# A hybrid attention and state-space layer: where the bias table is built, and which token group writes the split weights back to memory

## The chip, the cores and the metric

The kernel runs on one core of a Trainium2 chip. The core has a matrix engine (PE, with its weight loads listed as PEld), a vector engine (DVE), an activation engine (ACT), a general engine (POOL), a queue engine (SP) that issues nearly all transfers here, and 16 DMA engines that carry them out. The metric is the device time of one execution in microseconds (us), lower is better.

## The reference, cut to what matters

One decoder layer runs over a prompt of 2048 tokens and 8 sample tokens that share the weights. All matrices are float32.

```python
h = rms_norm(x, norm1_w)
proj = h @ w_in                              # 1024 -> 2312 columns: q, k, v, z, x/B/C, dt
a = swa_prompt(q, k, v, attn_sinks, rel_bias)   # window 128, adds rel_pos_bias to the scores
s_out = ssm_mixer(z, xbc, dt_raw, ...)          # conv, chunked scan, gate, grouped norm
x = x + concatenate([a, s_out]) @ w_out
h2 = rms_norm(x, norm2_w)
x = x + (silu(h2 @ w_gate) * (h2 @ w_up)) @ w_down   # hidden width 2816
y = rms_norm(x, final_norm_w)
```

`rel_pos_bias` looks up, for each head, one number per distance between query and key (0 to 127). All blocks of the prompt use the same 128 x 256 bias per head.

## The kernel before, in words

**Groups.** The tokens go through the layer in six groups, one after another: 256 tokens, four times 384, and 256 + 8. A token group is held with the features on the partitions, and every projection is a chain of matmuls with 128 x 128 pieces of weight as the stationary operand and 256 or 384 tokens as the moving one.

**Split weights.** Each product is made of three matmuls (`mm3`): a weight is split into a high part in a rounded format and the low rest, and so are the activations; high x high, high x low and low x high are added. `weight` (L189) hands out one unit of weight, 128 x 512 values (some units of `wd` are 128 x 384), as a tile `w2` of 128 x 1024 that holds both parts. There are 196 units: 36 of `wi`, 16 of `wo`, 44 each of `wg` and `wu`, 56 of `wd`. A unit's 4 pieces take 12 matmuls (9 for 384 columns). At the first use, in the first group, the raw unit (256 KB) is loaded into `wraw` (4 buffers), ACT copies it to the high part (L197), DVE or POOL in turn subtracts (L200), and two steps later the split tile (512 KB) is written to a buffer in memory (L202). The other five groups load the 512 KB (L193) and split nothing. `w2` has 5 buffers, so a unit's tile is free again when its matmuls are done and, in the first group, when its write has landed too.

**Bias table.** `setup_bias` (L140) multiplies a one-hot matrix with the table `rel_bias` and gets `tabl`, 8 heads (on 8 partitions) x 384 values. It writes each head's row 128 times to a buffer `bscr` in memory (L152), 1.5 MB in all, from those 8 partitions, and then loads each head's 128 x 256 bias with a row step of 383 (L157), by which each row is shifted by one. It is called after the stage K of the first group.

**Stages and order.** Each group goes through stages: X (norm; I for the first group), A (x/B/C and dt columns, conv), K (k and v columns), B (q and z columns), P and Q (attention and scan, "mixers", one block of 128 tokens after the other), S (mixer output split), O (output projection), H (norm), F (feed-forward), Z (final norm). The `run` calls at the end write the stages in an interleaved order: A(0), K(0), B(0) and the mixers of group 0, A(1), B(1), O(0), K(1), then F(0) with the mixers of group 1 beside it, K(2), A(2), O(1), B(2), F(1), and so on; groups are numbered from 0. `later` puts a piece of work some steps behind. The tile framework then places the instructions: it sorts each engine's instructions by a priority and a timing model of its own, hands out the buffers, and sets all waits. So a small edit moves rows on every engine. Each engine takes its own rows in order.

**Where the stages lie in the profiled execution** (from the weight loads that SP issues): the units of A(0), K(0), B(0) are loaded raw from 3.7 to 134.3 us, O(0) from 141.7 to 244.5, F(0) from 245.7 to 588.8; the next stages' loads are K(2), A(2), O(1), B(2) from 594.2 to 705.8, F(1) from 707.9 to 1012.9, F(2) from 1128.0 on.

Of the kernel before, what the change touches and what calls it, by code (L numbers as in the profile page):

```python
# [10 lines left out]
F32 = mybir.dt.float32  # L11
# [6 lines left out]
P = 128  # L18
# [13 lines left out]
NH = 8  # L32
EPS = 1e-6
NEG = -1e30
TW = 384
# [37 lines left out]
def hymba(ctx: ExitStack, tc: tile.TileContext, I: dict, O: dict, groups):  # L73
# [14 lines left out]
    def T(shape, dtype=F32, tag=None, bufs=1):  # L88
        cnt[0] += 1
        nm = f"{tag}_{cnt[0]}"  # L90
        return sb.tile(shape, dtype, tag=tag, name=nm, bufs=bufs)

    def PS(tag):
        cnt[0] += 1
        return pp.tile([P, 512], F32, tag=tag, name=f"ps{tag}_{cnt[0]}", bufs=4)

    def DR(shape, tag, bufs=1):
        cnt[0] += 1
        return dr.tile(shape, F32, tag=tag, name=f"{tag}_{cnt[0]}", bufs=bufs)

    V, S, G, PE, SP = nc.vector, nc.scalar, nc.gpsimd, nc.tensor, nc.sync

    def mm(o, l, r, start=True, stop=True):
        PE.matmul(o, l, r, start=start, stop=stop)  # L104
# [29 lines left out]
    def setup_consts():  # L134
        for c, w, e in ((S_CB, 40, AF.Copy), (S_A, NH, AF.Exp), (S_AR, 4, AF.Exp)):
            S.activation(cols[:, c:c + w], cols[:, c:c + w], e, scale=0.5 if e == AF.Copy else 1.0)
        V.tensor_scalar(Ab, Ab, -1.0, None, ALU.mult)
        V.tensor_scalar(Ar, Ar, -1.0, None, ALU.mult)

    def setup_bias():  # L140

        rb = T([33, NH], tag="rb")
        V.memset(rb, NEG)
        SP.dma_start(rb[0:32, :], I["rel"])
        ps = PS("m")
        oh = T([33, TW], tag="m2", bufs=M2)
        SP.dma_start(oh, I["consts"][0:33, C_OH:C_OH + TW])
        mm(ps[0:NH, 0:TW], rb, oh)
        tabl = T([NH, TW], tag="m2", bufs=M2)
        V.tensor_copy(tabl, ps[0:NH, 0:TW])  # L150
        bscr = DR([NH, P * TW], "bscr")
        SP.dma_start(bscr.rearrange("h (q w) -> h q w", w=TW),  # L152
                     tabl.unsqueeze(1).broadcast_to([NH, P, TW]))
        V.tensor_copy(sbias[:, 1:P], tabl[:, 128:255])
        V.tensor_copy(sbias[:, 0:1], tabl[:, 255:256])
        for h in range(NH):
            SP.dma_start(bias[:, h, :],  # L157
                         bscr[h, 0:P * (TW - 1)].rearrange("(q w) -> q w", w=TW - 1)[:, P - 1:P - 1 + 2 * P])
# [16 lines left out]
    def later(n, fn):  # L175
        due.append((clock[0] + n, len(due) + cnt[0] * 1e-6, fn))

    def tick():
        clock[0] += 1
        now = sorted((d for d in due if d[0] <= clock[0]), key=lambda d: d[:2])  # L180
        due[:] = [d for d in due if d[0] > clock[0]]
        for d in now:
            d[2]()

    wn, kept = [0], {}

    def weight(name, at, w=512):  # L189
        t = T([P, 1024], F32R, tag="w2", bufs=5)[:, :2 * w]  # L190
        hi, lo = t[:, :w], t[:, w:]
        if (name, at) in kept:
            SP.dma_start(t.bitcast(F32), kept[name, at])  # L193
            return hi, lo
        raw = T([P, 512], tag="wraw", bufs=4)[:, :w]
        SP.dma_start(raw, I[name][at] if name != "wd" else I[name][:, at:at + w])
        S.activation(hi, raw, AF.Copy)  # L197
        e = G if wn[0] % 2 else V
        wn[0] += 1
        e.tensor_tensor(lo, raw, hi.bitcast(F32), ALU.subtract)  # L200
        d = kept[name, at] = DR([P, 2 * w], f"{name}{len(kept)}")
        later(2, lambda: SP.dma_start(d, t.bitcast(F32)))  # L202
        return hi, lo

    def std(name, u):

        r = []
        for h in range(2):
            hi, lo = weight(name, (u, h))
            r += [(hi[:, k * P:(k + 1) * P], lo[:, k * P:(k + 1) * P]) for k in range(4)]  # L210
        return r
# [752 lines left out]
    def stage_f(g):  # L964
# [5 lines left out]
        def down(c, end=False):  # L970
            fs, n = chunks[c], len(chunks[c]) * P

            for ms in ([[0, 1, 2], [3], [4], [5], [6], [7]] if end else [[m] for m in range(KT)]):
                w = [weight("wd", c_off[c] + m * n, n) for m in ms]
                ps = [PS("d") for m in ms]
                jobs = [(i, m) for i in range(len(fs)) for m in range(len(ms))]
                for i, m in sorted(jobs, key=lambda e: (e[0] == len(fs) - 1, e[1], e[0])):
                    wi = tuple(t[:, i * P:(i + 1) * P] for t in w[m])
                    s = fs[i] % (FC + 1)
                    mm3(ps[m][:, :N], wi, (hid3[:, s], hid3[:, FC + 1 + s]), 0, N, i == 0, i == len(fs) - 1)  # L980
                for m, p in zip(ms, ps):
                    V.tensor_tensor(x1[:, m, :N], p[:, :N], x1[:, m, :N], ALU.add)  # L982
                    if end:
                        norm_sum(g, x1, sq, m, N, 0 if g is gs[-1] else 1)
                if ms[-1] % 4 == 3 or end:
                    yield
# [62 lines left out]
    def step(c, i):  # L1049

        if (c, i) not in made:
            made[c, i] = kinds[c](gs[i])
        return next(made[c, i], 0)

    def run(main, *rest, units=None, drain=99):


        rest = [e if isinstance(e, list) else [list(e[0]), e[1], 0.0] for e in rest]

        def advance(e, k):  # L1060
            e[2] += k
            while e[2] >= 1 and e[0]:
                if step(*e[0][0]) == 0:
                    e[0].pop(0)
                e[2] -= 1

        while units is None or units > 0:
            says = step(*main) if main else 0
            if says in (0, "tail"):
                break  # L1070
            tick()
            for e in rest:
                advance(e, e[1])
            if units is not None:
                units -= 1
        while any(e[0] for e in rest[:drain]):
            for e in rest[:drain]:
                e[2] = 0.0
                advance(e, 1)
            tick()  # L1080
        return rest[drain:]
# [6 lines left out]

    run(("I", 0), units=1)
    setup_consts()  # L1090
    run(("A", 0), ([("I", 0)], RI), units=UA)
    r = run(("A", 0), ([("X", 1)], RX1), drain=0)
    r = run(("K", 0), *r, drain=0)
    setup_bias()
    r = run(("B", 0), *r, units=UQ, drain=0)
    r = run(("B", 0), *r, *mixers(0, U0), drain=1)
    r = run(("A", 1), *r, drain=0)
# [112 lines left out]
```

## Time and profile before

| what | value |
|---|---|
| median of 3 runs | 2524.28 us (2523.79 to 2524.78) |
| the profiled execution's own time | 2512.29 us |
| its span, first to last instruction | 2510.5 us |
| mean granted TensorE clock | 0.974 |
| moved by DMA | 675.32 MB, 269 GB/s over the span |
| splits of weights | 196 on ACT, 98 on DVE, 98 on POOL |

A page of the profile gives one execution. A *window* row shows, for a stretch of time, the busy time of each engine with its instruction count, the clock that the matrix engine was granted (1.00 is full), the busy share of the 16 DMA engines and what they moved. A *waits* row names an engine and line, what it waited for, the total in us, how often, and the longest. A *timeline* row begins with start and length in us. In names, `psd<-bhi,w` is a write of `psd` from `bhi` and `w`.

### The profile page before, as it was taken

The numbers are of one execution on the slowest core, as the hardware profiler recorded it, in microseconds if no ns is written. First come the engines' busy times: TensorE is split into PE (matmuls) and PEld (weight loads), VectorE is DVE, ScalarE is ACT, GpSimd is POOL, SyncE is SP. The second block draws the span as 40 slices with busy tenths as digits, with TensorE's granted clock in tenths as the row PEclk, the third lists the DMA queues.
The fourth block names the chain that finished last, engine by engine and source line by source line (L and its number), as shares of the span: only waits on it lengthen the run. The fifth ranks groups of instructions, "written<-read, shape, count | busy, mean of one in ns | idle before, by whom it ended". The sixth has DMA issues, their size and how long they took to land.

```text
span 2510.5 us, 38909 instructions
## 1 busy us (share of the span) xinstructions
PE 2338.0 (93%) x14633; PEld 2264.2 (90%) x14633; DVE 1150.1 (46%) x2428; ACT 773.1 (31%) x1668; POOL 672.5 (27%) x787
## 2 busy tenths in 40 slices
PE   7499877878999999999999999999999999999997
PEld 6389876768999999999999999999999999999997
DVE  7384775634344543533453353445342655323223
ACT  5254544534232321432242233224132213112001
POOL 5233564434113221311321211222031323112000
PEclk8789999899999999999999999999999999999999
DMA  8678889799877777787777788767778788888997
GB/s 306 172 266 312 305 283 341 284 372 327 259 245 238 218 252 243 275 257 235 230 229 241 242 277 258 237 213 232 244 261 298 260 282 267 266 293 292 337 342 272
DMA packets 227054, 675.32 MB, mean 269 GB/s; under 512 B 24291, under 2 KB 51732, under 8 KB 226852
## 3 DMA queue, kind: packets, MB, share of 16 engines
q1 hardware_dynamic: 226724, 672.65, 80.1%
q8 instruction: 116, 1.90, 0.3%
q14 instruction: 70, 0.57, 0.1%
q10 hardware_dynamic: 144, 0.20, 0.0%
HBM read 563.07 MB, written 110.19 MB: 268 GB/s over the span
## 4 chain that ended last, share of the span: by engine, by line
PE 74%; DMA 11%; DVE 7%; ACT 3%; issue 2%; POOL 2%; SPq 1%; ACTq 0%; DVEq 0%; POOLq 0%
PE psd L104 69%; PE psm L104 4%; DMA w<-wd 2%; DMA w<-wi 2%; POOL w L200 1%; DMA xr<-in_xT_dram 1%; DVE w L200 1%; DMA wraw<-in_wd_dram 1%; DMA wu<-w 1%; DMA wraw<-in_wg_dram 1%; DMA w<-wg 1%; ACT w L197 1%; DVE big L726 1%; DMA w<-wu 1%; DVE xr L336 1%
## 5 line engine op out<-in xcount | busy, mean ns | idle before, releaser
L104 PE MATMUL psd<-bhi,w 128*128 128x384 f32 (+1 forms) x4448 | 1116.7, 331 | 91.5 <-ACT w L197 35.0
L104 PEld LDWEIGHTS psd<-bhi,w 128*128 128x128 f32 x4448 | 798.8, 194 | 114.4 <-ACT w L197 41.5
L104 PE MATMUL psd<-blo,w 128*128 128x384 f32 (+1 forms) x2224 | 725.8, 326 | 0.0
L104 PE MATMUL psd<-hc,w 128*128 128x384 f32 (+2 forms) x3168 | 525.6, 322 | 31.1 <-DMA w<-wd 8.1
L104 PEld LDWEIGHTS psd<-hc,w 128*128 128x128 f32 x3168 | 502.3, 191 | 44.0 <-DVE w L200 9.5
L104 PE MATMUL psd<-ahi,w 128*128 128x384 f32 (+1 forms) x2272 | 515.5, 314 | 17.8 <-DMA w<-wi 9.1
L104 PEld LDWEIGHTS psd<-blo,w 128*128 128x128 f32 x2224 | 431.9, 194 | 1.3
L104 PEld LDWEIGHTS psd<-ahi,w 128*128 128x128 f32 x2272 | 386.1, 189 | 25.9 <-issue 10.1
L104 PE MATMUL psd<-alo,w 128*128 128x384 f32 (+1 forms) x1136 | 354.9, 312 | 0.0
L982 DVE TENSOR_TENSOR x<-psd,x 128x384 f32<-128x384 f32 (+2 forms) x336 | 169.1, 511 | 229.9 <-PE psd L104 229.6
L104 PEld LDWEIGHTS psd<-alo,w 128*128 128x128 f32 x1136 | 215.0, 189 | 1.3
L1003 ACT ACTIVATE tmp<-psd 128x384 f32<-128x384 f32 (+2 forms) x132 | 59.9, 454 | 473.6 <-PE psd L104 473.2
L993 ACT ACTIVATE hc<-tmp 128x384 fp32r<-128x384 f32 (+2 forms) x132 | 64.6, 489 | 377.5 <-DVE tmp L992 368.7
L997 POOL TENSOR_TENSOR hc<-tmp,hc 128x384 fp32r<-128x384 f32 (+2 forms) x66 | 66.0, 1000 | 426.9 <-ACT hc L993 411.6
L309 POOL TENSOR_TENSOR sq<-sq,tmp 128x384 f32<-128x384 f32 (+2 forms) x112 | 107.4, 959 | 269.8 <-ACT tmp L306 265.1
L200 POOL TENSOR_TENSOR w<-wraw,w 128x512 fp32r<-128x512 f32 (+1 forms) x98 | 125.8, 1286 | 198.5 <-ACT w L197 165.5
L989 DVE SCALAR_TENSOR_TENSOR tmp<-tmp,psd 128x384 f32<-128x384 f32 (+2 forms) x132 | 66.7, 505 | 244.7 <-ACT tmp L1003 244.6
L992 DVE SCALAR_TENSOR_TENSOR tmp<-psd,tmp 128x384 f32<-128x384 f32 (+2 forms) x132 | 67.6, 512 | 225.3 <-PE psd L104 225.0
L197 ACT ACTIVATE w<-wraw 128x512 fp32r<-128x512 f32 (+1 forms) x196 | 114.9, 598 | 133.2 <-DMA wraw<-in_wi_dram 40.6
L200 DVE TENSOR_TENSOR w<-wraw,w 128x512 fp32r<-128x512 f32 (+1 forms) x98 | 82.2, 839 | 108.3 <-ACT w L197 104.5
L370 DVE SCALAR_TENSOR_TENSOR x<-tmp,cols,x 128x384 f32<-128x384 f32 (+1 forms) x144 | 90.8, 634 | 43.7 <-ACT x L392 32.9
L306 ACT ACTIVATE tmp<-x 128x384 f32<-128x384 f32 (+2 forms) x84 | 40.8, 490 | 171.2 <-DVE x L930 133.4
(269 smaller groups left out, 2109.4 us busy)
## 6 DMA issues: line engine op xcount, KB each, us to landing
w<-wg SPq DMA_DIRECT2D x220, 512.0 KB, 4.7
w<-wu SPq DMA_DIRECT2D x220, 512.0 KB, 4.4
w<-wi SPq DMA_DIRECT2D x180, 512.0 KB, 4.6
w<-wd SPq DMA_DIRECT2D x240, 384.0 KB, 3.7
w<-wo SPq DMA_DIRECT2D x80, 512.0 KB, 4.5
wg<-w SPq DMA_DIRECT2D x44, 512.0 KB, 4.9
wu<-w SPq DMA_DIRECT2D x44, 512.0 KB, 4.6
w<-wd SPq DMA_DIRECT2D x40, 512.0 KB, 4.3
```

The source lines that it names most:

```text
L104: PE.matmul(o, l, r, start=start, stop=stop)
L197: S.activation(hi, raw, AF.Copy)
L200: e.tensor_tensor(lo, raw, hi.bitcast(F32), ALU.subtract)
L306: S.activation(t[:, :N], x[:, m, :N], AF.Square)
L309: e.tensor_tensor(sq[:, :N], sq[:, :N], t[:, :N], ALU.add)
L370: V.scalar_tensor_tensor(acc, raw[:, j:j + NP], cwc(j, t), acc, ALU.mult, ALU.add)
L982: V.tensor_tensor(x1[:, m, :N], p[:, :N], x1[:, m, :N], ALU.add)
L989: V.scalar_tensor_tensor(t[:, :N], t[:, :N], 1.0, pg[:, :N], ALU.add, ALU.mult)
L992: V.scalar_tensor_tensor(t[:, :N], pu[:, :N], 0.5, t[:, :N], ALU.mult, ALU.mult)
L993: S.activation(hh[:, 0, :N], t[:, :N], AF.Copy)
L997: e.tensor_tensor(hl[:, 0, :N], t[:, :N], hh[:, 0, :N].bitcast(F32), ALU.subtract)
L1003: S.activation(t[:, :N], pg[:, :N], AF.Tanh, scale=0.5)
```

## The change

Two things are changed. First, `weight` counts for each unit how often it has been seen. Of the 196 units, taken in the order of first use, every third is written back at its first use, the next at its second and the third at its third. Until a unit has been written it is loaded raw (256 KB) and split anew, so 65 units are split once more and 65 twice more: 195 splits are added, and 195 loads of 512 KB become loads of 256 KB. The number of writes is the same; they lie a third each in the first three groups.

Second, `setup_bias` is called before A(0) and writes only the 12 KB table to memory (`tabd`). A new function `spread_bias` loads it into all 128 partitions (a tile of the ring `x1`, 12 KB per partition) and writes `bscr` from there; `load_bias` is the old loop over heads.

```diff
-        bscr = DR([NH, P * TW], "bscr")
-        SP.dma_start(bscr.rearrange("h (q w) -> h q w", w=TW),
-                     tabl.unsqueeze(1).broadcast_to([NH, P, TW]))
+        tabd = DR([NH, TW], "tabd")
+        SP.dma_start(tabd, tabl)
         V.tensor_copy(sbias[:, 1:P], tabl[:, 128:255])
         V.tensor_copy(sbias[:, 0:1], tabl[:, 255:256])
+        return tabd
+
+    def spread_bias(tabd):
+
+        t = T([P, NH, TW], tag="x1", bufs=2)
+        SP.dma_start(t, tabd.unsqueeze(0).broadcast_to([P, NH, TW]))
+        bscr = DR([NH, P * TW], "bscr")
+        SP.dma_start(bscr.rearrange("h (q w) -> q h w", w=TW), t)
+        return bscr
+
+    def load_bias(bscr):
         for h in range(NH):
...
-    wn, kept = [0], {}
+    wn, kept, seen = [0], {}, {}
...
-        d = kept[name, at] = DR([P, 2 * w], f"{name}{len(kept)}")
-        later(2, lambda: SP.dma_start(d, t.bitcast(F32)))
+        k = seen[name, at] = seen.get((name, at), len(seen) % 3) - 1
+        if k < 0:
+            d = kept[name, at] = DR([P, 2 * w], f"{name}{len(kept)}")
+            later(2, lambda: SP.dma_start(d, t.bitcast(F32)))
...
     setup_consts()
+    tabd = setup_bias()
     run(("A", 0), ([("I", 0)], RI), units=UA)
+    bscr = spread_bias(tabd)
     r = run(("A", 0), ([("X", 1)], RX1), drain=0)
     r = run(("K", 0), *r, drain=0)
-    setup_bias()
+    load_bias(bscr)
```

What follows are rows of the compiled programs, in the order in which an engine takes them (line, operation, output<-input, size). The names' numbers tell buffers apart.

SP in B(0), before, where the bias buffer is written: between raw loads (L196) and write-backs (L202) of `wi` stand the write of `bscr` and, a few rows on, the loads of `bias`.

```order
L196 DMA wraw_897<-in_wi_dram 128x512
L202 DMA wi_160_847<-w_158_842 128x1024
L152 DMA bscr_737<-m_140_735 1024x1x384
L196 DMA wraw_939<-in_wi_dram 128x512
L261 DMA xr_2771<-in_xT_dram 128x4x384 x2
L196 DMA wraw_945<-in_wi_dram 128x512
L202 DMA wi_163_853<-w_161_848 128x1024
L202 DMA wi_168_895<-w_166_890 128x1024
```

The same steps of SP in the changed program, now in A(0): the load of the table into 128 partitions (L160), the write (L162) and the loads of `bias` (L167).

```order
L206 DMA wraw_440<-in_wi_dram 128x512
L160 DMA x_47_295<-tabd_123 128x3072
L206 DMA wraw_445<-in_wi_dram 128x512
L206 DMA wraw_496<-in_wi_dram 128x512
L214 DMA wi_67_392<-w_65_387 128x1024
L206 DMA wraw_502<-in_wi_dram 128x512
L206 DMA wraw_549<-in_wi_dram 128x512
L162 DMA bscr_297<-x_47_295 128x8x384
L206 DMA wraw_554<-in_wi_dram 128x512
L214 DMA wi_87_500<-w_85_495 128x1024
L206 DMA wraw_612<-in_wi_dram 128x512
```

The write moved from stage B(0) to stage A(0), the load of the table stands five rows ahead of it, and the eight loads of `bias` six rows behind it.

SP in F(0), before: raw loads and write-backs of `wg` and `wu` take turns.

```order
L202 DMA wg_693_3733<-w_691_3728 128x1024
L196 DMA wraw_3838<-in_wg_dram 128x512
L202 DMA wg_696_3739<-w_694_3734 128x1024
L196 DMA wraw_3844<-in_wg_dram 128x512
L202 DMA wu_703_3788<-w_701_3783 128x1024
L196 DMA wraw_3895<-in_wu_dram 128x512
L202 DMA wu_706_3794<-w_704_3789 128x1024
L196 DMA wraw_3901<-in_wu_dram 128x512
```

SP in F(0), in the changed program.

```order
L206 DMA wraw_3310<-in_wg_dram 128x512
L206 DMA wraw_3315<-in_wg_dram 128x512
L214 DMA wu_582_3269<-w_580_3264 128x1024
L206 DMA wraw_3370<-in_wu_dram 128x512
L206 DMA wraw_3375<-in_wu_dram 128x512
L206 DMA wraw_3433<-in_wg_dram 128x512
L206 DMA wraw_3439<-in_wg_dram 128x512
L214 DMA wg_591_3319<-w_589_3314 128x1024
```

Two or three raw loads now stand between two write-backs.

DVE in O(1), before: the eight column blocks of the output projection are added to `x` (L930) with only conv rows (L370, L381) between.

```order
L370 SCALAR_TENSOR_TENSOR x_1182_6285<-tmp_6613,cols_68,x_1182_6285 128x384 x2
L930 TENSOR_TENSOR x_1226_6624<-psd_6632,x_1226_6624 128x384
L381 SCALAR_TENSOR_TENSOR x_1182_6285<-tmp_6659,x_1182_6285 128x384
L930 TENSOR_TENSOR x_1226_6624<-psd_6666,x_1226_6624 128x384
L930 TENSOR_TENSOR x_1226_6624<-psd_6699,x_1226_6624 128x384
L930 TENSOR_TENSOR x_1226_6624<-psd_6732,x_1226_6624 128x384
```

DVE in O(1), in the changed program: the same adds are L942, and L210 is the split. On PE the tile `w_1167_6615` belongs to the block whose sum is `psd_6621`.

```order
L942 TENSOR_TENSOR x_1146_6493<-psd_6505,x_1146_6493 128x384
L393 SCALAR_TENSOR_TENSOR x_1092_6130<-tmp_6532,x_1092_6130 128x384
L210 TENSOR_TENSOR w_1167_6615<-wraw_6616,w_1167_6615 128x512
L942 TENSOR_TENSOR x_1146_6493<-psd_6543,x_1146_6493 128x384
L942 TENSOR_TENSOR x_1146_6493<-psd_6584,x_1146_6493 128x384
L210 TENSOR_TENSOR w_1177_6688<-wraw_6689,w_1177_6688 128x512
L942 TENSOR_TENSOR x_1146_6493<-psd_6621,x_1146_6493 128x384
L210 TENSOR_TENSOR w_1185_6730<-wraw_6731,w_1185_6730 128x512
```

The second group now splits between the adds; the split of the second unit for `psd_6621` stands behind the add of the block three before it.

## The prediction

> **What bounds the kernel now.** I read the slices first, then windows by stage, then who waits for whom in the slow stages. The slices of 63 us (rows PE, PEclk and DMA of the page) show two regimes.
>
> ```profile
> PE   7499877878999999999999999999999999999997
> PEclk8789999899999999999999999999999999999999
> DMA  8678889799877777787777788767778788888997
> PE 74%; DMA 11%; DVE 7%; ACT 3%; issue 2%; POOL 2%; SPq 1%; ACTq 0%; DVEq 0%; POOLq 0%
> ```
>
> From slice 10 on PE is full; there only less matmul work would help. The first nine slices (about 600 us) hold PE's idle time, and the last row, the chain that ended last, has 26% off PE. The change moves work out of just these slices and into later ones. By stage:
>
> ```profile
> 26.00:83.00 57.00, 39.03 (x238) 34.35 (x238) 49.01 (x89) 32.99 (x68) 33.55 (x39) 0.84 0.82 298
> 83.00:119.00 36.00, 10.25 (x60) 9.79 (x59) 5.08 (x12) 3.65 (x7) 4.52 (x3) 0.59 0.62 117
> 119.00:142.00 23.00, 16.56 (x86) 14.00 (x86) 15.00 (x44) 8.27 (x17) 8.60 (x7) 0.65 0.87 320
> 142.00:217.00 75.00, 74.69 (x453) 71.26 (x453) 54.61 (x131) 43.12 (x103) 27.69 (x47) 0.97 0.76 254
> 217.00:264.00 47.00, 43.01 (x291) 41.48 (x290) 14.05 (x28) 20.50 (x40) 17.30 (x17) 0.96 0.94 360
> 264.00:330.00 66.00, 57.02 (x411) 52.91 (x409) 60.07 (x115) 35.40 (x84) 45.46 (x45) 0.95 0.79 275
> 264.00:595.00 331.00, 265.40 (x1823) 240.12 (x1822) 204.96 (x377) 156.50 (x339) 170.66 (x164) 0.93 0.87 317
> 708.00:1013.00 305.00, 303.03 (x1801) 299.22 (x1800) 132.77 (x289) 80.85 (x180) 67.85 (x78) 1.00 0.74 232
> 1128.00:1430.00 302.00, 300.60 (x1786) 296.69 (x1785) 131.68 (x286) 80.31 (x178) 68.03 (x78) 1.00 0.74 233
> ```
>
> The columns are length, then busy us of PE, PEld, DVE, ACT, POOL, then clock, DMA share, GB/s. F(0) (264 to 595) works on 256 tokens and takes 331 us; F(1) and F(2) work on 384 and take 305 and 302. Two thirds of the tokens cost more time, with DMA at 317 GB/s against 232: this is the write-back of the split weights. And in 83 to 119 PE stands nearly still while DMA moves only 117 GB/s.
>
> **The change part by part.** *Bias write.* SP's timeline and, below, PE's:
>
> ```profile
> 83.14 0.81 SPq L152 DMA_DIRECT2D bscr<-m  x1
> 84.00 10.49 SPq L196 DMA_DIRECT2D wraw<-in_wi_dram  x1
> 94.61 9.48 SPq L261 DMA_DIRECT2D xr<-in_xT_dram  x2
> 104.18 7.79 SPq L196 DMA_DIRECT2D wraw<-in_wi_dram  x1
> ...
> 118.36 0.58 PE L104 MATMUL psd<-bhi,w 128*128 128x256 f32 x1 [23.32 <-ACT w L197]
> ...
> 86.00:94.00 8.00, 5.56 (x38) 5.39 (x36) 2.14 (x4) 2.09 (x4) 1.57 (x2) 0.84 0.47 52
> ```
>
> Behind the write of `bscr` one raw load takes 10.49 us to issue, the next transfers 9.48 and 7.79, and PE waits 23.32 us for the split of a unit that came late. The last row, eight us in which the write runs nearly alone, has a DMA share of 0.47: half of the 16 engines work, at 52 GB/s. The write leaves from the 8 partitions of `tabl`. The changed one leaves from 128 partitions; at the 298 GB/s of the row 26 to 83 its 1.5 MB take 5 us, the new load of 1.5 MB another 5, under DMA that loses two thirds of its writes there. Gain: PE's idle time in 83 to 119 is 36 - 10.25 = 26 us, and I take it whole, 26; it is at least 12, if the 10 us of transfers and a wait are paid openly, and at most 36, if the slow clock of the two rows (0.59 and 0.65 of 27 us busy, so 10 us) goes too. The Trainium skill, "DMA: Bandwidth & Descriptors" (section "Why a DMA increments its semaphore by 16 and not by 1"), says that the number of engines is the largest up to 16 that divides the outermost dimension of both sides: 8 for the old write, which the 0.47 bears out, 16 for the new one, which no row here shows.
>
> New waits: the load of the table waits for its 12 KB write, the `bscr` write for that load, the `bias` loads for that write; behind each on SP stand raw loads of `wi`. The order has 5 to 10 other transfers between them, and four raw buffers are ahead, so I price them at 0; uncovered they cost one landing each, 4 to 8 us, three times, which the 12 above holds. Table and matmul move ahead at two more issues of under 1 us.
>
> *Write-backs out of F(0).* First what F(0) would take with PE never idle. Starts on PE at full clock, three matmuls of 256 columns apart, and a window of pure 384-column work:
>
> ```profile
> 89.00 0.40 PE L104 MATMUL psd<-bhi,w 128*128 128x256 f32 x2
> ...
> 89.36 0.40 PE L104 MATMUL psd<-bhi,w 128*128 128x256 f32 x2
> ...
> 640.00:674.00 34.00, 34.00 (x198) 34.00 (x197) 10.02 (x19) 7.55 (x15) 4.72 (x8) 1.00 0.83 252
> ```
>
> That is 0.12 us each at 256 and 34/198 = 0.172 at 384. F has 96 units of 12 matmuls and 48 of 9, 1584 in all. F(1): 1584 x 0.172 = 272 of its 305 us, 33 for the mixers of three blocks. F(0) has mixers of three blocks too: 1584 x 0.12 + 33 = 223 us. So 331 - 223 = 108 us is lost. What it waits for (PE, then SP, in F(0)):
>
> ```profile
> PE psd L104 <- DVE w L200: 23.6, 18, 7.5
> PE psd L104 <- POOL w L200: 22.7, 32, 1.4
> PE psd L104 <- ACT w L197: 10.0, 16, 3.0
> ...
> SPq L202 <- POOL w L200: 47.6, 33, 4.4
> SPq L202 <- DVE w L200: 37.5, 17, 8.3
> SPq L196 <- DVE w L200: 32.2, 14, 6.4
> ...
> L197 ACT ACTIVATE w<-wraw 128x512 fp32r<-128x512 f32 x95 | 58.7, 625 | 50.9 <-DMA wraw<-in_wg_dram 18.2 <-DMA wraw<-in_wu_dram 17.2 <-PE psd L104 9.9
> L200 POOL TENSOR_TENSOR w<-wraw,w 128x512 fp32r<-128x512 f32 x47 | 63.5, 1353 | 91.6 <-ACT w L197 74.0 <-DMA wraw<-in_wd_dram 7.1 <-PE psd L104 6.1
> L200 DVE TENSOR_TENSOR w<-wraw,w 128x512 fp32r<-128x512 f32 x48 | 41.0, 854 | 52.2 <-ACT w L197 52.0
> ```
>
> PE waits for splits, DVE and POOL for ACT, ACT for raw data, and SP, which must bring the data, stands 85 us in front of write-backs (L202) until splits are done. A ring: a write-back in SP's row holds up the raw loads behind it. In the change a unit moves 256 KB and a third of 512, 427 KB against 768; F(0)'s 331 us x 317 GB/s = 105 MB become some 61, at its own 317 GB/s 193 us, below 223. So DMA no longer binds. The splits stay, 144 in F(0). Next late is DVE with 205 us of work. PE was full with DVE at 54.61/75 = 73% and reached 57.02/66 with DVE at 91%; between, at 82%, DVE's 205 us take 250. Forecast F(0) 250, gain 81. Ends: 223 (gain 108); and if PE's waits for splits, 23.6 + 22.7 + 10.0 = 56 us, all stay, 279 (gain 52). O(0), 217 to 264, where DMA is at 0.94, gives back up to its 4 idle us: 3.
>
> *195 splits in groups 1 and 2.* Each is 0.6 us on ACT and 0.85 on DVE or 1.35 on POOL. The first 24 or so fall into 142 to 217, where PE is full and DVE has 20 us free: 12 x 0.85 = 10 on DVE; I charge 3. In F(1) 96 splits add 41 us to DVE's 133, 65 to POOL's 68 and 60 to ACT's 81, all far below 303; bytes there are equal (512 KB per unit on average), in F(2) 597 KB, so its share 0.74 becomes 0.86, still under the 0.94 of O(0). Cover is there, and in the order a split stands some four units (8 us) ahead of its matmuls. If the cover is gone a split costs what it cost in F(0): 56/144 = 0.39 us, 195 times, 76 us. I take 10, near the lower end 0, by the busy rows.
>
> The longest and shortest splits bear on this:
>
> ```profile
> L200 DVE TENSOR_TENSOR w<-wraw,w x98: 545/692/1785, 12.0 to 592.9; 128x512 fp32r<-128x512 f32 x74, 128x384 fp32r<-128x384 f32 x24
> ```
>
> A DVE split takes 692 ns in the middle and up to 1785. The Trainium skill, "SBUF — State Buffer" (section "Who interferes with whom"), says that a DVE instruction with two inputs in SBUF and a GpSimd instruction that reads SBUF shut each other out for a whole instruction; the 1785 is about 692 plus a POOL split, so the trace agrees. It speaks against more POOL splits. By it DVE in 142 to 217 would need 54.6 + 10 + 12 x 1.35 = 81 us of 75, and the sum would be 6 us worse; in F(1) DVE stays under 240 of 303.
>
> **Sum.** -26 - 81 - 3 + 3 + 10 = -97 us. The profiled execution took 2512.3 us (span 2510.5), so 2415. The runs' median, 2524.28, lies 12 us (0.5%) above it; against the median the forecast is **2427**.
>
> **The rivals.** (1) *F(0) stays bound by the split chain* ACT, DVE or POOL, PE: the 56 us of PE's waits stay, and F(0) gains 52. For it: these waits name the splits, not the DMA. Against: ACT itself waits for raw data. Time 2427 + 29 = 2456. (2) *PE becomes the bound*: F(0) at 223 to 228 and the slow clock at 83 to 142 gone: 27 + 8 less, 2392. (3) *The bias costs as much elsewhere*, at the raw loads of A(0): 14 less gain, 2441; the free DMA share speaks against it. (4) *Slower*: in groups 1 and 2 splits hold up a PE that is now full; ACT takes its rows in order, so a split that waits for one of the five `w2` buffers, held by a write-back, holds up the activations behind it. At 0.39 us each it costs 76, not enough; it decides from (97 + 10)/195 = 0.55 us per split on. At the 0.71 us that a PE wait for POOL took in F(0) (22.7/32) it costs 138: 2524 + 138 - 107 = 2555. Against it stand the busy rows of F(1). That the change does nothing can't be: the order shows the write-backs gone.
>
> **How the numbers follow.** Forecast with its neighbourhood (2405 to 2447) 0.60, rival 1 0.15, rival 2 0.12, rival 3 0.06, rival 4 0.07. The range takes in rivals 1 to 3 and the milder part of the split cost: 2388 to 2476. A measurement of this kernel tells 0.2% (5 us) from no change. Slower 0.05, within 0.2% 0.02, faster 0.93: rival 4 ends on either side of nothing, but mostly slower.
>
> **What would show it.** Right: no SP issue of over 3 us behind the `bscr` write and no PE wait of 20 us before 142; F(0) near 250 us with the SP waits of L202 small; F(1) and F(2) within 5 us of 305 and 302 with PE over 98% busy. Wrong: F(0) over 280 with PE's waits for splits still near 56 us; PE waiting for ACT, DVE or POOL splits in F(1) or F(2); a new wait of raw loads at the table's transfers; DMA share near 0.95 in F(2).

## The result, and the profile after

| | before | after |
|---|---|---|
| median of 3 runs | 2524.28 us | 2439.97 us (2437.1 to 2444.46) |
| ratio, 95% interval | | 0.9668 [0.9644, 0.9692] |
| profiled execution, its span | 2512.29, 2510.5 us | 2437.1, 2434.7 us |
| mean granted TensorE clock | 0.974 | 0.985 |
| moved by DMA | 675.32 MB | 628.97 MB |

The kernel became 3.3% faster: 84 us by the medians, 76 us between the two profiled executions. From the page of the changed kernel, the slices of PE, of its clock and of DMA (61 us each):

```profile
PE   6889898999999999999999999999999999999997
PEclk9899998999999999999999999999999999999999
DMA  8648575787776777878788887777789788888997
```

All of PE's digits but the first and the last are now 8 or 9, where there were a 4 and several 7s in the first nine, while DMA in the second to eighth slice has come down to 4 to 7 tenths, but for one 8. Then the windows of the changed kernel (length, busy PE, PEld, DVE, ACT, POOL, clock, DMA share, GB/s), with one more window of before behind them:

```profile
83.00:119.00 36.00, 32.45 (x223) 29.14 (x224) 29.62 (x70) 18.78 (x50) 16.22 (x17) 0.90 0.69 228
248.00:495.00 247.00, 217.71 (x1643) 201.48 (x1642) 185.82 (x343) 134.76 (x294) 152.63 (x142) 0.97 0.67 220
232.00:512.00 280.00, 244.15 (x1816) 226.22 (x1816) 212.42 (x378) 156.30 (x342) 178.25 (x164) 0.96 0.66 217
624.00:929.00 305.00, 302.62 (x1782) 297.57 (x1781) 172.56 (x335) 129.50 (x271) 130.00 (x126) 0.99 0.71 234
1042.00:1348.00 306.00, 302.70 (x1790) 297.16 (x1789) 146.31 (x310) 105.83 (x225) 98.33 (x102) 1.00 0.79 265
```

```profile
280.00:575.00 295.00, 233.80 (x1608) 209.62 (x1608) 178.45 (x339) 133.57 (x290) 145.48 (x140) 0.94 0.87 317
```

In 83 to 119, where PE was busy 10 us and DMA moved 117 GB/s, PE is now busy 32 us. F(1) (624 to 929) and F(2) (1042 to 1348) carry the added splits in DVE, ACT and POOL and are about as long as before (305 and 302 us), PE over 98% busy. The row 232 to 512 is the counterpart of the prediction's F(0) row (264 to 595): both begin 16 to 17 us ahead of F(0)'s first gate activation and hold nearly the same number of matmuls (1816 and 1823).

To compare stages between kernels I use the gate's activation (tanh), 22 of them in each F: from the first to the last start. In before and in the changed kernel, F(0) begins and ends with these rows of ACT's timeline:

```profile
280.03 0.37 ACT L1003 ACTIVATE tmp<-psd 128x256 f32<-128x256 f32 x1
...
574.99 0.39 ACT L1003 ACTIVATE tmp<-psd 128x256 f32<-128x256 f32 x1 [2.08 <-PE psd L104]
```

```profile
248.78 0.37 ACT L1015 ACTIVATE tmp<-psd 128x256 f32<-128x256 f32 x1
...
494.19 0.37 ACT L1015 ACTIVATE tmp<-psd 128x256 f32<-128x256 f32 x1
```

| from timeline, us | before | after | gain |
|---|---|---|---|
| start to first tanh of F(0) | 280.0 | 248.8 | 31.2 |
| F(0), first to last tanh | 295.0 | 245.4 | 49.6 |
| to the first tanh of F(1) | 145.4 | 137.7 | 7.7 |
| F(1) | 279.4 | 282.3 | -2.9 |
| F(2) | 278.8 | 282.1 | -3.3 |
| everything else | 1231.9 | 1238.4 | -6.5 |

So the gain lies before 500 us. The 6.5 us of "everything else" lie mostly in F(4) (298.9 and 301.6) and F(5) (189.9 and 192.2), where the changed kernel splits nothing; no run here says why. What PE's own work in F(0) is worth on this scale can be estimated: F(3) takes 277.0 in both kernels with PE full, (277 - 33)/0.172 = 1419 matmuls, at 0.12 us 170, with the mixers' 33 it is 203. Before, 92 us were lost above that, now 42. These 42 are the question of most experiments.

### The profile page after: what moved, and what is told of

Its sections match the earlier page's. It is cut to its first block, busy times and chain, and to the rows that moved or that the text cites. A ratio compares the mean times of both kernels' runs of the same rounds, so it can differ in the third digit from the quotient of the medians.

```text
span 2434.7 us, 39664 instructions
## 1 busy us (share of the span) xinstructions
PE 2314.5 (95%) x14633; PEld 2244.4 (92%) x14633; DVE 1250.4 (51%) x2526; ACT 875.1 (36%) x1861; POOL 814.4 (33%) x884
## 2 busy tenths in 40 slices
DMA packets 227227, 628.97 MB, mean 258 GB/s; under 512 B 24323, under 2 KB 57916, under 8 KB 226892
## 4 chain that ended last, share of the span: by engine, by line
PE 68%; DMA 7%; DVE 2%; ACT 1%; issue 0%; SPq 0%; ACTq 0%; POOL 0%; DVEq 0%
PE psd L104 64%; PE psm L104 4%; DMA w<-wd 2%; DMA w<-wi 2%; DMA w<-wu 1%; DMA w<-wg 1%; DVE x L1042 1%; DVE xr L348 1%; DVE alo L339 0%; DMA out_yT_dram<-x 0%; DMA m<-sbcd 0%; PE psm L608 0%; PE psm L728 0%; DVE w L210 0%; ACT L696 0%
## 5 line engine op out<-in xcount | busy, mean ns | idle before, releaser
L104 PE MATMUL psd<-bhi,w 128*128 128x384 f32 (+1 forms) x4448 | 1097.4, 328 | 40.0 <-DVE w L210 14.9
L104 PEld LDWEIGHTS psd<-bhi,w 128*128 128x128 f32 x4448 | 785.6, 190 | 54.6 <-DVE w L210 19.1
L104 PEld LDWEIGHTS psd<-blo,w 128*128 128x128 f32 x2224 | 423.2, 190 | 2.8 <-DVE blo L339 1.1
L104 PEld LDWEIGHTS psd<-ahi,w 128*128 128x128 f32 x2272 | 386.1, 189 | 31.2 <-DMA w<-wi 5.0
L210 POOL TENSOR_TENSOR w<-wraw,w 128x512 fp32r<-128x512 f32 (+1 forms) x195 | 252.7, 1298 | 382.1 <-ACT w L207 346.3
L207 ACT ACTIVATE w<-wraw 128x512 fp32r<-128x512 f32 (+1 forms) x391 | 232.5, 601 | 324.4 <-PE psd L104 187.7
L994 DVE TENSOR_TENSOR x<-psd,x 128x384 f32<-128x384 f32 (+2 forms) x336 | 168.0, 510 | 193.9 <-PE psd L104 193.4
L210 DVE TENSOR_TENSOR w<-wraw,w 128x512 fp32r<-128x512 f32 (+1 forms) x196 | 164.4, 840 | 90.7 <-ACT w L207 88.6
L382 DVE SCALAR_TENSOR_TENSOR x<-tmp,cols,x 128x384 f32<-128x384 f32 (+1 forms) x144 | 100.3, 700 | 37.2 <-ACT x L404 26.7
```

The costliest lines, as they stand in the source:

```text
L382: V.scalar_tensor_tensor(acc, raw[:, j:j + NP], cwc(j, t), acc, ALU.mult, ALU.add)
```

## The experiments

All ratios are to the kernel before on the same chip. The first four rows share one set of runs of before (median 2521.22), the next four another (2520.82), the last four a third (2519.9).

| run | median us | ratio, interval | start to F(0) | F(0) | F(1) |
|---|---|---|---|---|---|
| changed kernel again | 2435.07 | 0.9656 [0.9633, 0.9678] | 248.8 | 243.3 | 283.5 |
| bias part only | 2504.03 | 0.9938 [0.9918, 0.9958] | 265.4 | 293.9 | 279.6 |
| weight part only | 2457.07 | 0.9744 [0.9721, 0.9766] | 268.0 | 245.6 | 282.7 |
| no write-back in the first group | 2414.95 | 0.9575 [0.9554, 0.9596] | 242.6 | 228.9 | 288.0 |
| DVE a third of the first splits | 2452.36 | 0.9720 [0.9695, 0.9745] | 251.4 | 257.9 | 282.6 |
| bias spread at its old place | 2429.86 | 0.9637 [0.9602, 0.9672] | 247.0 | 244.7 | 283.3 |
| bias early, from 8 partitions | 2454.34 | 0.9725 [0.9706, 0.9744] | 269.3 | 242.1 | 283.0 |
| 3 raw buffers | 2478.61 | 0.9820 [0.9797, 0.9843] | 261.1 | 268.5 | 282.1 |
| DVE two thirds of them | 2420.47 | 0.9605 [0.9580, 0.9630] | 244.3 | 231.1 | 282.5 |
| 5 raw buffers | 2412.17 | 0.9571 [0.9548, 0.9594] | 247.9 | 221.2 | 281.3 |
| 5, and no write-back in the first group | 2410.99 | 0.9572 [0.9550, 0.9594] | 241.8 | 223.0 | 284.3 |
| never written back | 2430.76 | 0.9642 [0.9627, 0.9657] | 243.7 | 228.9 | 283.9 |

**The changed kernel again**, unedited: 

> The changed kernel once more, on the chip of the other runs, so that they can be compared with it directly: 2440 us, ratio 0.967, give or take 0.3%.

 It came out as expected.

**The two parts apart.** The bias part alone, with the write-back of before:

```diff
-        k = seen[name, at] = seen.get((name, at), len(seen) % 3) - 1
-        if k < 0:
-            d = kept[name, at] = DR([P, 2 * w], f"{name}{len(kept)}")
-            later(2, lambda: SP.dma_start(d, t.bitcast(F32)))
+        d = kept[name, at] = DR([P, 2 * w], f"{name}{len(kept)}")
+        later(2, lambda: SP.dma_start(d, t.bitcast(F32)))
```

> Only the bias part of the change; all split weights are written in the first group, as before. Theory: the two parts are separate terms, and the bias part is worth the 26 us that PE lost behind the write from 8 partitions. No PE wait of 20 us before 142 us, first to last gate activation (tanh) of F(0) stays at 295 us as before; time 2499 us, ratio to before 0.990. Rival: in A(0) and B(0) the write-backs bind anyway, the wait is paid elsewhere; gain of 10 us or less, 2514 us or more, ratio 0.996.

And the weight part alone: the kernel before with these four lines the other way round.

> Only the weight part of the change; the bias table is written from 8 partitions, in its old place. Theory: first to last gate activation of F(0) is 245 us as in the changed kernel (295 before), the wait of PE of some 20 us behind the bias write is still there; time 2465 us, ratio 0.977, and the gains of this run and of the bias part alone add up to the change's 84 us within 8. Rival: with fewer write-backs the bias write no longer blocks, the parts overlap: 2450 us or less, and the two gains add up to over 95 us.

PE's waits up to 145 us, of the bias part alone and below of the weight part alone (total us, times, longest), with the row of PE's timeline behind the longest one:

```profile
PE psd L104 <- DVE w L210: 14.6, 8, 5.0
PE psd L104 <- ACT w L207: 13.5, 8, 3.1
PE psd L104 <- POOL w L210: 5.2, 4, 2.8
```

```profile
PE psd L104 <- DMA w<-wi: 23.6, 1, 23.6
PE psd L104 <- DVE w L200: 13.5, 7, 6.1
...
122.71 0.69 PE L104 MATMUL psd<-ahi,w 128*128 128x384 f32 x1 [23.56 <-DMA w<-wi]
```

The weight part alone did what was expected, in 8 us less than the 2465 forecast: F(0) at 245.6, a single wait of 23.6 us left behind the write of `bscr`, now for a reload of `wi` for the second group (its matmuls have 384 columns). This run also begins F(0) 12 us earlier than before (268.0 against 280.0). The bias part removed the long wait, but alone gave 0.62% or 16 us, between the theory's 26 and the rival's 10: 33 us of waits for splits are left (14.6 + 13.5 + 5.2), none of them long. In before the same three waits were 46 us (29.5 + 12.7 + 3.8), the long one of 23.3 in them, so some 10 of its 23 us were paid again in short waits, as the rival had it in part. That raw loads still share SP and the DMA engines with all write-backs is the likely reason; it has no run of its own. On top of the weight part the bias part gives 0.9744 - 0.9656 = 0.88%, 22 us. The single gains, 16 and 65 us, add up to 80 of the 87 on this chip: two terms, nearly separate.

**Which half of the bias edit counts.** Spread, but at the old place (all three bias steps called after K(0)):

```diff
-    tabd = setup_bias()
     run(("A", 0), ([("I", 0)], RI), units=UA)
-    bscr = spread_bias(tabd)
     r = run(("A", 0), ([("X", 1)], RX1), drain=0)
     r = run(("K", 0), *r, drain=0)
-    load_bias(bscr)
+    load_bias(spread_bias(setup_bias()))
```

> The changed kernel, with the whole bias table made, spread over the partitions and written where it was before, after the stage K of the first group. Theory: the write from 8 partitions was what cost, its place does not matter; no wait of PE over 10 us before 145 us, first gate activation of F(0) within 5 us of 249, time within 6 us of the changed kernel on this chip. Rival: the place matters, since 4 MB of transfers now stand in front of the raw loads of B(0); first gate activation at 258 us or later, time 10 us or more above the changed kernel.

Early, but written from the 8 partitions of the table:

```diff
-        tabd = DR([NH, TW], "tabd")
-        SP.dma_start(tabd, tabl)
+        bscr = DR([NH, P * TW], "bscr")
+        SP.dma_start(bscr.rearrange("h (q w) -> h q w", w=TW),
+                     tabl.unsqueeze(1).broadcast_to([NH, P, TW]))
...
-    bscr = spread_bias(tabd)
```

> The changed kernel, with the bias table made early but written from its 8 partitions. Theory that the 8 partitions cost: the wait of PE moves to before 70 us and stays at 15 us or more, first gate activation of F(0) at 262 us or later, time 13 to 22 us above the changed kernel. Rival, place alone: within 5 us of the changed kernel.

The row of SP's timeline behind the early write, and PE's longest wait up to 145 us in the same run; below them SP's rows of the changed kernel in the same place:

```profile
14.72 0.79 SPq L152 DMA_DIRECT2D bscr<-m  x1
16.07 13.89 SPq L207 DMA_DIRECT2D wraw<-in_wi_dram  x2
...
PE psd L104 <- ACT w L208: 27.3, 4, 25.9
```

```profile
23.98 0.33 SPq L160 DMA_DIRECT2D x<-tabd  x1
28.75 4.78 SPq L206 DMA_DIRECT2D wraw<-in_wi_dram  x2
33.62 0.38 SPq L214 DMA_DIRECT2D wi<-w  x1
34.05 1.78 SPq L206 DMA_DIRECT2D wraw<-in_wi_dram  x2
35.92 0.40 SPq L162 DMA_DIRECT2D bscr<-x  x1
40.44 0.33 SPq L206 DMA_DIRECT2D wraw<-in_wi_dram  x1
```

Early from 8 partitions, SP again needs 13.89 us for two raw loads and PE waits 25.9 us, only at another time; the run is 0.7% slower than the changed kernel by the ratios. Spread at the old place is as fast as the changed kernel (0.9637 against 0.9656, the intervals overlap). With the weight part in all of them, the four combinations are: 8 partitions 0.9744 (old place) and 0.9725 (early), 128 partitions 0.9637 (old place) and 0.9656 (early). So the write from 8 partitions is what cost, and the place is worth nothing that can be measured. No run tells the number of partitions from what changes with it: the old write reads each row 128 times, the new one reads 128 copies once. One thing the prediction priced at nothing does show in the rows above: behind the load of the table two raw loads take 4.78 us to issue.

**What is left in F(0).** The prediction held that DMA no longer binds there and DVE comes next. First, no write-back at all in the first group:

```diff
-        k = seen[name, at] = seen.get((name, at), len(seen) % 3) - 1
+        k = seen[name, at] = seen.get((name, at), len(seen) % 2 + 1) - 1
```

> The change, but with no write-back in the first group: half of the split weights are written in the second group and half in the third (98 more splits than in the changed kernel). Theory: what is left over PE's own time in F(0) of the changed kernel (about 50 us) is not the remaining third of the write-backs but engines that take their rows in order, DVE first; F(0) from first to last gate activation stays within 8 us of 245, time 2440 us give or take 8. Rival: the remaining write-backs still hold the raw loads; F(0) falls to 225 us and the time to 2420.

The theory fell: F(0) dropped to 228.9 and the time by 0.8% to 2415. DVE did the same work in it at a higher share. From the windows and the DMA issues (last column: median us to landing) of this run, and from the DMA issues of before and of the changed kernel in F(0):

```profile
242.00:472.00 230.00, 208.14 (x1617) 199.10 (x1616) 188.85 (x341) 134.68 (x294) 153.52 (x142) 0.96 0.47 147
wraw<-in_wg_dram SPq DMA_DIRECT2D x38, 256.0 KB, 2.9
wraw<-in_wd_dram SPq DMA_DIRECT2D x48, 192.0 KB, 2.5
```

```profile
wraw<-in_wg_dram SPq DMA_DIRECT2D x38, 256.0 KB, 4.6
wraw<-in_wd_dram SPq DMA_DIRECT2D x48, 192.0 KB, 4.0
```

```profile
wraw<-in_wg_dram SPq DMA_DIRECT2D x38, 256.0 KB, 3.6
wraw<-in_wd_dram SPq DMA_DIRECT2D x48, 192.0 KB, 3.2
```

DVE is at 189/230 = 82%, the very share that the forecast had taken, at 230 us and not at 250, while the changed kernel had 186/247 = 75%. And a raw load of `wg` lands after 4.6, 3.6, 2.9 us with all, a third and none of the write-backs, although the DMA share of the latter two is only 0.67 and 0.47. Who waits in F(0) of the changed kernel, SP first, then ACT:

```profile
SPq L206 <- DVE w L210: 50.7, 21, 8.2
SPq L206 <- POOL w L210: 44.9, 35, 3.6
```

```profile
ACT w L207 <- DMA wraw<-in_wg_dram: 22.9, 14, 3.6
ACT w L207 <- DMA wraw<-in_wd_dram: 20.8, 17, 2.3
ACT w L207 <- DMA wraw<-in_wu_dram: 19.9, 15, 2.6
```

SP spends 96 us before a raw load (L206), until DVE or POOL is done with an older raw buffer, and ACT 64 us until raw data land. The waits alone prove little, since ACT waited 56 us so in before as well (21.0 + 18.2 + 17.2), in a longer F(0). They suggest a ring of 4 raw buffers, held up by its round trip: issue, landing, ACT, DVE or POOL, free again. The other ring, the five `w2` tiles that a write-back holds until it lands, does not show: none of ACT's waits in this F(0) ends with a landed write-back. The new theory was tested from four sides. Fewer buffers:

```diff
-        raw = T([P, 512], tag="wraw", bufs=4)[:, :w]
+        raw = T([P, 512], tag="wraw", bufs=3)[:, :w]
```

> The changed kernel with 3 instead of 4 buffers for raw weights. Theory of the raw ring: where it binds, a unit's time grows by a third; first to last gate activation of F(0) rises from 245 to 270 us or more, and the time to 2460 or more. Rival, that SP's place behind the write-backs or DVE binds F(0): F(0) stays within 8 us of 245, the time within 10 us of the changed kernel.

More of them, with `M2 = 7` for the room:

> The changed kernel with 5 instead of 4 raw buffers; the 2 KB per partition are taken from the ring m2 of the mixers (7 instead of 8). Raw ring theory: the fifth buffer gives less than the loss of the fourth cost (23 us in F(0), 12 before it), F(0) falls to 230 to 240 us, the time by 8 to 20 us. Rival: with four buffers the ring no longer binds by much, and the smaller m2 costs as much as the fifth raw buffer gives: within 5 us of the changed kernel, or slower.

And the holding time: DVE does a split faster than POOL, so its share of the first group's splits was cut to a third, and in another run raised to two thirds.

```diff
-        e = G if wn[0] % 2 else V
+        first = (name, at) not in seen
+        e = (V if wn[0] % 3 == 0 else G) if first else G if wn[0] % 2 else V
```

> The changed kernel, with DVE doing a third instead of half of the splits of the first group (about 24 of F(0)'s 72 move to POOL). The theory that DVE's row of work binds F(0) in the changed kernel: DVE loses 20 us there, first to last gate activation falls from 245 to 235 us or less, time 2425 us. The new theory, after the run without write-backs in the first group: the ring of the 4 raw buffers binds (a raw load waits for a buffer, ACT for the raw data, the buffer for DVE or POOL); POOL takes 1.3 us where DVE takes 0.85, so F(0) does not fall, 243 to 255 us, time 2433 to 2445.

> The changed kernel, with DVE doing two thirds instead of half of the splits of the first group. If the raw ring binds F(0), the faster split (0.85 us on DVE, 1.3 on POOL) frees a raw buffer sooner and F(0) falls by 3 to 10 us below 245, the time by as much. If DVE's row binds, which has 20 us more to do, F(0) rises by 5 us or more.

ACT's waits for raw data in F(0) with 3 and then with 5 buffers; below the latter that run's window of F(0), its landing of `wg` and PE's longest waits in it:

```profile
ACT w L207 <- DMA wraw<-in_wd_dram: 32.1, 25, 3.3
ACT w L207 <- DMA wraw<-in_wg_dram: 30.0, 21, 3.1
ACT w L207 <- DMA wraw<-in_wu_dram: 22.6, 17, 3.3
```

```profile
ACT w L207 <- DMA wraw<-in_wu_dram: 10.6, 9, 2.7
ACT w L207 <- DMA wraw<-in_wg_dram: 6.6, 7, 1.7
ACT w L207 <- DMA wraw<-in_wd_dram: 5.4, 6, 1.5
...
248.00:469.00 221.00, 205.91 (x1605) 196.22 (x1604) 182.77 (x341) 133.51 (x292) 155.11 (x141) 0.97 0.74 242
wraw<-in_wg_dram SPq DMA_DIRECT2D x38, 256.0 KB, 3.9
PE psd L104 <- DVE tmp L1001: 7.0, 2, 4.4
PE psm L104 <- DVE m L622: 4.0, 1, 4.0
```

All four went the ring's way. With 3, 4 and 5 buffers F(0) takes 268.5, 245.4 and 221.2 us and ACT waits 85, 64 and 23 us for raw data. With 5 buffers a raw load of `wg` lands no earlier (3.9 us against 3.6), which points to the number of loads in flight, and not to the landing alone. With less work on DVE F(0) became longer (257.9), with more shorter (231.1), and with 5 buffers DVE is at 183/221 = 83%: DVE's share is not what binds at 245. The ring does not bind all the time either: if it did, 3 buffers would have made F(0) a third longer, 327 us. The sizes were not all met: the run with 3 buffers stayed just under its 270, and the other three moved F(0) further than their ranges (12.5 us up, where at most 10 was expected; 14 down for 10; 24 down for 15). The smaller `m2` had no run of its own, so its part in that 24 is open.

Both cures together, in the lines shown above:

> No write-back in the first group and 5 raw buffers (m2 has 7). The two act on the same ring, so they add up in part: F(0) 218 to 226 us against 229 with no write-back alone, time 5 to 12 us below that run. Rival: F(0) is at the matrix engine's own 203 us plus what the in-order engines cost, no change to the run without write-backs, 2410 to 2420 us.

F(0) is 223.0, 6 us under the run without write-backs and inside the theory's 218 to 226; but the time did not fall with it (0.9572 against 0.9575, 2411 us), as the rival had said. Against 5 buffers alone (221.2 and 2412) nothing is added: with a fifth buffer the remaining third of the write-backs costs nothing in F(0) that shows. These two and the run without write-backs in the first group are the fastest kernels here, 0.957 of before and about 0.9% under the changed kernel.

**What a split costs where PE is full.** The start value 99 in place of `len(seen) % 3` lets no unit ever be written.

> The change carried to its end: no unit is ever written back, all six groups load raw weights and split them (980 splits more than before the change, no write-back, half the bytes read per unit). If a split costs PE nothing where PE is full, F(1) to F(3) stay within 3 us of 282 by first to last gate activation, F(0) is 229 as without write-backs, the time 2400 to 2425 us. If each split costs PE 0.1 us or more in the later groups, F(1) to F(3) take 295 us or more, and the time is 2480 or more.

F(1) to F(3) take 283.9, 281.6 and 278.3 us with 144 splits each, against 279.4, 278.8 and 277.0 before with none: 1 to 5 us, or 0.01 to 0.03 us per split. In the changed kernel, where F(1) and F(2) also carry a third of the write-backs each, it is 2.9 us for 96 splits and 3.3 for 48, so 0.03 and 0.07. F(5), the last group with 264 tokens, got shorter, 179.4 us against 189.9. Its window in this run, and below it the one of before:

```profile
2219.00:2398.00 179.00, 174.66 (x1440) 174.19 (x1439) 96.49 (x178) 93.98 (x180) 90.87 (x79) 0.99 0.61 186
```

```profile
2292.00:2482.00 190.00, 180.07 (x1444) 175.79 (x1444) 49.05 (x112) 20.96 (x47) 7.57 (x10) 1.00 0.95 339
```

There the reload of 512 KB per unit had DMA at 0.95; raw loads bring it to 0.61. F(4), with the sample tokens' work beside it, lost 10 us (308.9 against 298.9), 0.07 per split. The whole stays 0.7% behind the run with no write-back in the first group, so keeping the split weights is worth something in some stages and costs in the last.

## Why the prediction was right, and which term was off

The forecast was 2427 us, the result 2440, inside the range. Between the profiled executions, on which the sum was built, it is 76 us of 97; the medians give 84, because the profiled execution of before lay 12 us under its median and that of the changed kernel 3. By the sum's own terms:

- **Bias write, 26 us.** The mechanism is shown: the 23 us wait is gone only where the write leaves from 128 partitions, and comes back with 8 wherever it stands. The new waits cost nothing that shows: the run with all of them late is no slower. The size was too large for the edit (16 us alone, 22 on top of the weight part): taking all of PE's idle time in 83 to 119 left no room for the short waits on splits, of which 10 us came back.
- **O(0) and 142 to 217, -3 and +3.** Together with the bias term the forecast had 26 us up to F(0); the profile shows 31.2. That they are close is partly luck: of the 31.2, the weight part alone gives 12.0, where the sum had 0, and the bias part 19.2 on top of it (268.0 to 248.8), where it had 26.
- **F(0), 81 us.** Here the sum was mis-sized: 331 us became 280 by the prediction's own windows, a gain of 51; by the activations it is 49.6 in F(0) and 7.7 until F(1), 57. The step that failed is "So DMA no longer binds ... Next late is DVE", with DVE's 205 us at 82% giving 250. DVE had 212 us of work in the 280, 76%. What the runs show in its place: SP's waits for splits in front of write-backs did become small, 13 us (10.3 + 3.1) against 69 (40.0 + 28.5) before, so the mechanism is there; but raw loads still land later with a third of the write-backs than with none, and a ring of four raw buffers turns that into time while DVE has room. How much of the rest is the later landing, and how much SP's remaining 22 us in front of write-backs, no run tells. A share of 82 or 83% for DVE was reached without write-backs and with a fifth buffer, at 230 and 221 us. Rival 1 named the chain (ACT, DVE or POOL, PE) and put F(0) at 279, a gain of 52, which is what came; but PE's direct waits for splits fell to 11.5 of the 56 us that it rested on, so its number was right by luck and its reason was not. PE's longest wait in total is not for a split but for DVE's adds of the down projection (L994, 8.3 us); with 5 buffers that wait is gone too. So DVE has a part in F(0), though not the one that the forecast gave it. These are PE's longest waits in F(0) of the changed kernel:

```profile
PE psd L104 <- DVE x L994: 8.3, 5, 2.5
PE psd L104 <- DVE w L210: 4.9, 8, 1.0
PE psd L104 <- ACT ahi L345: 4.8, 1, 4.8
PE psd L104 <- ACT w L207: 4.0, 4, 2.6
PE psd L104 <- POOL w L210: 2.6, 6, 0.6
```

- **195 splits, 10 us.** F(1) and F(2) lost 2.9 and 3.3 us, PE stayed over 98% busy. The cover was there; rival 4 needed 0.55 us per split, and no stage of a run here shows more than 0.07. Another 6.5 us were lost elsewhere, mostly in F(4) and F(5), for which the sum had no term.
- **Rival 3**, a gain of only 12 us on the bias, was nearer than the forecast for the bias part alone (16), but not for the change (22). **Rival 2**, PE as the bound in F(0), was not reached by any run: 221 us is the shortest, against the estimate of 203. PE is busy 206 of these 221 us; 11 of the 15 idle ones are waits for DVE's work on the gate and in the mixers (7.0 and 4.0 in the rows of that run), so there DVE does come next. No run tests that.

That DVE and POOL hold each other up, which the prediction weighed, is not settled by these runs. DVE's splits of 128 x 384 in F(0) take 984 ns on average in the changed kernel and 713 where POOL does a third of the splits instead of half; but with POOL at half they take 869 in the unedited run of the changed kernel and 768 with 5 buffers, and those of 128 x 512 take 886 with POOL at half and 845 with POOL at two thirds.

## What to carry to other kernels

A stage whose DMA share is well below one (0.67 here) can still be held up by transfers: divide the round trip of a buffer (issue, landing, all who read it) by the number of buffers and compare it with the time that a unit of work may take. An estimate for the changed F(0): 3.6 us to landing, 0.6 for ACT's copy and 0.9 or 1.4 for the split are 5.1 to 5.6 us, by four buffers 1.3 to 1.4 per unit, while PE's own work leaves 203/144 = 1.4: no room for delay. When writes are taken away, look at how fast the reads now land and how long their buffers are held, before naming the busiest engine as the next bound. In this kernel a write of 1.5 MB from 8 partitions held up the transfers behind it on its queue at both places where it was issued; spreading it through memory first cost less than it saved.

## What was not expected of the hardware

More splits on DVE did not make DVE busier in F(0): 21 more of them (87 against 66 in the windows used), moved over from POOL, and its busy time was 180.44 us, against 185.82 in the changed kernel (window of 247 us):

```profile
244.00:475.00 231.00, 210.37 (x1615) 200.20 (x1614) 180.44 (x362) 134.03 (x292) 125.08 (x119) 0.95 0.71 233
```

The fall is no more than what the unedited changed kernel shows from one execution to the next: run again, it had 180.90 us in its F(0). With half of the splits on DVE the runs here lie between 173 and 189. What surprises is that 21 more splits of 0.7 us or more, some 15 us, do not show. Why stays open.

Two thirds of the splits on DVE were also 0.5% faster than half of them (0.9605 against 0.9656 in another set of runs, the intervals lie just apart), a gain without any buffer.
